# Two-stream modulations as products on TensorE in a bank of their own, loads two steps ahead, five banks in the long feed forwards, Toeplitz products interleaved

## The chip, the cores and the metric

The kernel runs on one core of one Trainium2 chip. The metric is the device time of one execution in microseconds (us); less is better.

## The reference

Four layers (pool, attention, state space, gated MLP), each followed by a convolutional feed forward. Each of the layers takes six modulation vectors out of one matrix product with the conditioning vector, and in the first two layers the latent stream of 256 positions and the context stream of 256 positions both run through everything; in the last two only the latent stream does.

```python
sh1, sc1, gt1, sh2, sc2, gt2 = ada_modulations(c, ada_w[layer], ada_b[layer])      # silu(c) @ w + b, split in 6
csh1, csc1, cgt1, csh2, csc2, cgt2 = ada_modulations(c_ctx, ada_w[layer], ada_b[layer])
...
x_lat = post_norm_residual(x_lat, y_lat, gt1, ln1_g[layer], ln1_b[layer])
f_lat = conv_ffn(modulate(x_lat, sh2, sc2), ffn_w_up[layer], ffn_conv_w[layer], ffn_conv_b[layer], ffn_w_down[layer])
...
def conv_ffn(h, w_up, conv_w, conv_b, w_down):
    a = h @ w_up                                   # [n, 1024] @ [1024, 5632]
    a = conv_b + ap[:, 0:n] * conv_w[0] + ...      # three taps along the positions
    val, gate = a[..., :FFN_HIDDEN], a[..., FFN_HIDDEN:]
    return (val * jax.nn.silu(gate)) @ w_down      # [n, 2816] @ [2816, 1024]
```

`ada_w` is 4 x 1024 x 6144 and all of it has to be read. The state-space layer (64 groups of 16 channels, 64 complex states, both directions) is computed by the kernel as long convolutions in blocks. Their kernels are made beforehand from the layer's parameters; one part of that, for each of 8 blocks of channels and each half of 4 groups, is a set of small products, the Toeplitz products.

## The kernel before

**Matrix products.** Each float32 product is done as three reduced products of a high and a low part (`mm3`, lines 223 to 225; `hH`, `hL` are the parts of the activations, `wH`, `wL` those of the weights). A weight block of 128x1024 is loaded into `raw`, ScalarE writes `wH` (line 164), VectorE or GpSimd the difference `wL` (line 165).

**The feed forward** (`ffn`) goes over 11 pairs of 128 hidden channels, in three parts. For each pair, 4 accumulators of one bank each (`ps`; value half `vi` 0 and gate half `vi` 1, each of two channel tiles) take 96 ordinary products of 512 columns. Behind them stand the convolution (ScalarE's Identity on line 1794, VectorE's lines 1795 and 1797, all from the bank into `cv`), Silu, the product of the halves on GpSimd (line 1801) and the split into `gH`, `gL`. After each part come the down products, whose results VectorE adds through `tmp` (lines 406 and 407). The banks of PSUM are shared out by `banks(n)`: 6 for `ps`, two (`bg`) for background work. Each of the two stages for layers 0 and 1 has 66 weight blocks; after each block's load stands a `hook`.

**Background work.** At each hook, `bg` takes steps of two lists, by a rate. The first list are modulation tasks (l, m) (`ada_task`): one step loads 128 rows of one of the six blocks of `ada_w` (`araw`, 512 KB). Task (0,5) multiplies them on TensorE (`products`, line 310: four column groups of 32, 256 columns each, which the trace counts as 8 records). Tasks of layers 1 to 3 instead sum on VectorE, with the conditioning value as scalar (line 323 for the first step, line 325 for the others, once for each stream, into `adaS`), and products with a vector of ones close the sum. Tasks (1,0) to (1,4) fall into the first feed forward, (1,5) and (2,0) to (2,4) into the second. The second list prepares the state-space layer (`ssm_tasks`): GpSimd makes complex products `ef` and `efp` (lines 1160 to 1167), from which `toeplitz` makes one call of products for each of 8 blocks and 2 halves.

**Order.** The program's order of writing is not the order on the engines: a scheduler with a cost model of its own lists the instructions of each engine, and each engine then works its list in order. Waits for data and for free buffers come on top.

In the middle of the first pair of a long feed forward, `turn_second` transposes the second stream (`turn`), with banks from the same six.

Of the kernel before, what the change touches and what calls it, by code (L numbers as in the profile page):

```python
# [65 lines left out]
class Trunk:  # L66
    def __init__(self, ctx, tc, I, out, out_ctx=None, layers=(0, 1, 2, 3)):
# [3 lines left out]
        self.pp, self.bgp, self.held, self.ada, self.begun = [], None, [], {}, set()  # L71
# [35 lines left out]
    def banks(self, n, bg=2):  # L107


        self.flush()  # L110
        for pool in reversed(self.held):
            pool.release()
        self.held, self.pp, self.bgp, self.psn = [], [], None, 0
        self.more_banks(0, bg)
        self.more_banks(n)

# [8 lines left out]
    def flush(self):  # L125

        if self.bg_ada and self.bg_ada[0][0] in self.begun and not self.alone(*self.bg_ada[0][0]):
            self.need(self.bg_ada[0][0])
# [164 lines left out]


# [3 lines left out]
    def ada_task(self, l, m, place=None, scale=None, vec=None, bank=None, apart=False):  # L298
# [6 lines left out]
        bank = bank or (lambda: self.ps(True))  # L305
        vec = not l == 0 if vec is None else vec
        ps = None
        def products(lhs, rhs, start, stop):
            for q in range(4):
                nc.tensor.matmul(ps[32 * q:32 * q + 32, 0:256], lhsT=lhs, rhs=rhs[:, q * 256:(q + 1) * 256], start=start, stop=stop)  # L310
        two = vec and not self.alone(l, m)
        acc = [self.t(self.sm, [128, D], F32, "adaS", 2) for r in range(1 + two)] if vec else None
        for k in range(KT):
            raw = place(128)
            self.last_load = nc.sync.dma_start(raw, I["ada_w"][l, k * 128:(k + 1) * 128, m * D:(m + 1) * D])
            if acc is None:
                ps = ps or bank()
                products(self.cond[:, k, :], raw, k == 0, k == KT - 1 and not gate)
            else:
                with self.tc.issue_after(self.last_hT.ins):  # L320
                    for r, a in enumerate(acc):
                        if k == 0:
                            nc.vector.tensor_scalar(a, raw, self.cond[:, k, r:r + 1], None, op0=ALU.mult)
                        else:
                            nc.vector.scalar_tensor_tensor(a, raw, self.cond[:, k, r:r + 1], a, op0=ALU.mult, op1=ALU.add)  # L325
            if k < KT - 1:
                yield
# [200 lines left out]
    def turn(self, r):  # L528

        pss = []  # L530
        for kk in range(4):
            if kk == 2 and r:

                self.psn -= 2
# [794 lines left out]
    def ssm_pre(self, k, pp, eng, behind):  # L1329
# [33 lines left out]
        def toeplitz(hb, f):  # L1363
            nc.sync.dma_start(self.fD[k, :, hb], f.rearrange("p r n -> p (r n)"))
            pk = [self.ps(True), self.ps(True)]
            for q in range(4):
                g = 4 * hb + q
                rows = slice(32 * q, 32 * q + 32)
                lhs = lambda i, hp: pr[hp, self.XB + i * 128 + g * 16:self.XB + i * 128 + g * 16 + 32]
                for i in range(2):  # L1370
                    mm(pk[0][rows, 0:112], lhsT=lhs(i, slice(64, 128)), rhs=f[64:128, i, q * 128 + 16:q * 128 + 128], start=i == 0, stop=i == 1)
                for i in range(2):
                    mm(pk[1][rows, 128:240], lhsT=lhs(i, slice(0, 64)), rhs=f[0:64, i, q * 128:q * 128 + 112], start=i == 0, stop=i == 1)
                for i in range(2):
                    mm(pk[1][rows, 112:128], lhsT=lhs(i, slice(0, 128)), rhs=cs[:, i, g], start=i == 0, stop=False)
# [377 lines left out]
    def ffn(self, l, last):  # L1753
# [8 lines left out]
        with tc.tile_pool(name=f"ffn{l}", bufs=2) as fp:  # L1762
            for part, pairs in enumerate(parts):
                gs = []
                for p in pairs:
# [3 lines left out]
                    pss = [[self.ps() for j in range(2)] for vi in range(2)]  # L1769
                    ws = {}  # L1770

                    for r, vi in ((0, 0), (0, 1), (1, 1), (1, 0))[:2 * S] if p == 0 else ((None, 0), (None, 1)):
# [12 lines left out]
                    cw = cw or self.conv(l)  # L1785
                    for j in range(2):
                        hid = 2 * p + j
                        cv = []
                        for vi in range(2):
                            ps = pss[vi][j]  # L1790
                            h = hid + vi * NHT
                            c = self.t(fp, [128, S, 256], F32, f"cv{vi}", 2)
                            p3 = ps[:, :T].rearrange("p (s n) -> p s n", s=S)
                            nc.scalar.activation(c, p3, AF.Identity, scale=cw[:, 1, h:h + 1], bias=cw[:, 3, h:h + 1])  # L1794
                            nc.vector.scalar_tensor_tensor(c[:, :, 1:], p3[:, :, :255], cw[:, 0, h:h + 1], c[:, :, 1:],  # L1795
                                                           op0=ALU.mult, op1=ALU.add)
                            nc.vector.scalar_tensor_tensor(c[:, :, :255], p3[:, :, 1:], cw[:, 2, h:h + 1], c[:, :, :255],  # L1797
                                                           op0=ALU.mult, op1=ALU.add)
                            cv.append(c)
                        nc.scalar.activation(cv[1], cv[1], AF.Silu)  # L1800
                        nc.gpsimd.tensor_tensor(cv[0], cv[0], cv[1], op=ALU.mult)  # L1801
                        gH = self.t(fp, [128, T], F32R, "gH", 8)
                        gL = self.t(fp, [128, T], F32R, "gL", 8)
                        c0 = cv[0].rearrange("p s n -> p (s n)")
# [103 lines left out]
    def run(self):  # L1908
# [10 lines left out]
        for l in ls:  # L1919
# [3 lines left out]
            if l < 2 and todo:  # L1923
                self.rate, self.until = ((0.85, 0.85)[l], 2.0), (l + 1, 4)
# [5 lines left out]
            if l == 2 and 3 in ls:  # L1930
                self.gmlp_open()
            self.ffn(l, l == ls[-1])
# [33 lines left out]
```

## Time and profile before

| | |
|---|---|
| Median of three runs | 1969.92 us (1967.69 to 1974.09) |
| The profiled execution's own time | 1976.77 us |
| Its span in the trace | 1975.0 us |
| TensorE (PE) busy | 1796.1 us, 91% of the span |
| VectorE (DVE) busy | 1489.5 us, 75% |
| GpSimd (POOL) busy | 1131.2 us, 57% |
| ScalarE (ACT) busy | 780.9 us, 40% |
| Mean granted clock of TensorE | 0.953 |

The shares are means over stages that differ. The first feed forward runs from about 80 to 545 us, the second from about 760 to 1215 us. In the rows, PE is TensorE's matmuls and PEld its weight loads, L310 is line 310 of the kernel, and `a<-b,c` says which tile is written from which.

### The profile page before, as it was taken

The numbers are of one execution on the slowest core, as the hardware profiler recorded it, in microseconds if no ns is written. First come the engines' busy times: TensorE is split into PE (matmuls) and PEld (weight loads), VectorE is DVE, ScalarE is ACT, GpSimd is POOL, SyncE is SP. The second block draws the span as 40 slices with busy tenths as digits, with TensorE's granted clock in tenths as the row PEclk, the third lists the DMA queues.
The fourth block names the chain that finished last, engine by engine and source line by source line (L and its number), as shares of the span: only waits on it lengthen the run. The fifth ranks groups of instructions, "written<-read, shape, count | busy, mean of one in ns | idle before, by whom it ended". The sixth has DMA issues, their size and how long they took to land.

```text
span 1975.0 us, 31117 instructions
## 1 busy us (share of the span) xinstructions
PE 1796.1 (91%) x11804; PEld 1496.4 (76%) x11804; DVE 1489.5 (75%) x1981; ACT 780.9 (40%) x1288; POOL 1131.2 (57%) x1040
## 2 busy tenths in 40 slices
PE   6899999898999998988999998679898988979997
PEld 4787787676788877766877677448897968979997
DVE  4676997895777767978866546987889798778666
ACT  3252243124346643332432232234544544436553
POOL 1477218999763326852168996756654554236543
PEclk9899999998999999999999999888999999989999
DMA  9465665654321122546655647775878856447652
GB/s 354 165 195 185 204 213 166 202 177 136 106 90 32 44 88 55 202 125 208 223 195 202 208 138 232 209 220 181 277 259 270 279 198 210 156 144 268 212 183 86
DMA packets 241784, 360.25 MB, mean 182 GB/s; under 512 B 43353, under 2 KB 164825, under 8 KB 241634
## 3 DMA queue, kind: packets, MB, share of 16 engines
q1 hardware_dynamic: 241634, 358.26, 56.0%
q8 instruction: 93, 1.52, 0.3%
q14 instruction: 57, 0.47, 0.1%
HBM read 330.92 MB, written 27.29 MB: 181 GB/s over the span
## 4 chain that ended last, share of the span: by engine, by line
PE 27%; POOL 13%; DVE 9%; DMA 6%; issue 3%; ACT 1%; SPq 0%; POOLq 0%; DVEq 0%; ACTq 0%
PE ps L225 8%; PE ps L223 8%; PE ps L224 8%; DMA araw<-in_ada_w_dram 2%; DVE wL L165 2%; DVE adaS L325 1%; DMA raw<-in_ffn_w_up_dram 1%; POOL cv L1801 1%; POOL ef L1165 1%; POOL efp L1166 1%; POOL ef L1160 1%; POOL ef L1162 1%; POOL efp L1161 1%; POOL ef L1167 1%; POOL wL L165 1%
## 5 line engine op out<-in xcount | busy, mean ns | idle before, releaser
L223 PE MATMUL ps<-hH,wH 128*128 128x256 f32 (+1 forms) x1568 | 525.4, 337 | 26.2 <-DVE cv L1797 9.6
L225 PE MATMUL ps<-hH,wL 128*128 128x256 f32 (+1 forms) x1568 | 520.4, 333 | 7.4 <-DVE wL L165 7.4
L224 PE MATMUL ps<-hL,wH 128*128 128x256 f32 (+1 forms) x1568 | 522.0, 333 | 0.8 <-DVE hL L512 0.7
L164 ACT ACTIVATE wH<-raw 128x1024 fp32r<-128x1024 f32 x341 | 358.0, 1056 | 400.5 <-PE ps L225 190.9
L165 DVE TENSOR_TENSOR wL<-raw,wH 128x1024 fp32r<-128x1024 f32 x292 | 424.8, 1461 | 114.0 <-ACT wH L164 104.1
L223 PEld LDWEIGHTS ps<-hH,wH 128*128 128x128 f32 x1568 | 305.2, 195 | 59.3 <-issue 12.6
L225 PEld LDWEIGHTS ps<-hH,wL 128*128 128x128 f32 x1568 | 304.8, 195 | 35.6 <-DVE wL L165 8.6
L224 PEld LDWEIGHTS ps<-hL,wH 128*128 128x128 f32 x1568 | 305.9, 195 | 26.5 <-POOL xa L617 0.9
L325 DVE SCALAR_TENSOR_TENSOR adaS<-araw,cond,adaS 128x1024 f32<-128x1024 f32 x182 | 282.8, 1572 | 42.4 <-DMA araw<-in_ada_w_dram 42.0
L1801 POOL TENSOR_TENSOR cv<-cv,cv 128x512 f32<-128x512 f32 (+1 forms) x88 | 119.2, 1360 | 224.8 <-ACT cv L1800 218.1
L224 PE MATMUL ps<-wL,gH 128*128 128x512 f32 (+1 forms) x552 | 216.4, 393 | 11.9 <-DVE wL L165 11.9
L223 PE MATMUL ps<-wH,gH 128*128 128x512 f32 (+1 forms) x552 | 216.6, 395 | 5.9 <-DVE tmp L406 5.5
L225 PE MATMUL ps<-wH,gL 128*128 128x512 f32 (+1 forms) x552 | 211.8, 391 | 4.4 <-DVE gL L1806 3.8
L165 POOL TENSOR_TENSOR wL<-raw,wH 128x1024 fp32r<-128x1024 f32 x49 | 125.1, 2555 | 115.1 <-ACT wH L164 97.4
L1794 ACT ACTIVATE cv<-ps,cw 128x512 f32<-128x512 f32 (+1 forms) x176 | 115.3, 665 | 139.8 <-PE ps L225 104.7
L1795 DVE SCALAR_TENSOR_TENSOR cv<-ps,cw,cv 128x510 f32<-128x510 f32 (+1 forms) x176 | 106.0, 608 | 62.3 <-ACT cv L1794 59.6
L224 PEld LDWEIGHTS ps<-wL,gH 128*128 128x128 f32 x552 | 105.6, 191 | 36.2 <-DVE wL L165 14.7
L223 PEld LDWEIGHTS ps<-wH,gH 128*128 128x128 f32 x552 | 105.5, 191 | 32.2 <-DVE tmp L406 6.0
L225 PEld LDWEIGHTS ps<-wH,gL 128*128 128x128 f32 x552 | 105.2, 191 | 28.7 <-DVE gL L1806 4.9
L524 POOL TENSOR_SCALAR rs<-mv 128x1 f32<-128x1 f32 x26 | 8.2, 314 | 176.1 <-DVE mv L522 175.8
L1797 DVE SCALAR_TENSOR_TENSOR cv<-ps,cw,cv 128x510 f32<-128x510 f32 (+1 forms) x176 | 105.9, 611 | 3.0
L1805 ACT ACTIVATE gH<-cv 128x512 fp32r<-128x512 f32 (+1 forms) x88 | 45.8, 522 | 131.7 <-POOL cv L1801 131.7
(414 smaller groups left out, 3471.7 us busy)
## 6 DMA issues: line engine op xcount, KB each, us to landing
araw<-in_ada_w_dram SPq DMA_DIRECT2D x184, 512.0 KB
raw<-in_ffn_w_up_dram SPq DMA_DIRECT2D x176, 512.0 KB
raw<-in_ffn_w_down_dram SPq DMA_DIRECT2D x88, 512.0 KB
raw<-in_gmlp_w_in_dram SPq DMA_DIRECT2D x32, 512.0 KB
fD<-ef SPq DMA_DIRECT2D x16, 512.0 KB
eD<-eo SPq DMA_DIRECT2D x16, 512.0 KB
raw<-in_gmlp_w_out_dram SPq DMA_DIRECT2D x16, 512.0 KB
raw<-in_attn_w_qkv_dram SPq DMA_DIRECT2D x12, 512.0 KB
```

Source lines behind the costliest of these rows:

```text
L164: self.nc.scalar.activation(h, x, AF.Copy)
L165: (eng or self.nc.vector).tensor_tensor(l, x, h.bitcast(F32), op=ALU.subtract)
L223: mm(ps, lhsT=w[0], rhs=x[0], start=first, stop=False)
L224: mm(ps, lhsT=w[0], rhs=x[1], start=False, stop=False)
L225: mm(ps, lhsT=w[1], rhs=x[0], start=False, stop=last)
L325: nc.vector.scalar_tensor_tensor(a, raw, self.cond[:, k, r:r + 1], a, op0=ALU.mult, op1=ALU.add)
L1160: eng.tensor_tensor(out[0], a[0], b[0], op=ALU.mult)
L1794: nc.scalar.activation(c, p3, AF.Identity, scale=cw[:, 1, h:h + 1], bias=cw[:, 3, h:h + 1])
L1795: nc.vector.scalar_tensor_tensor(c[:, :, 1:], p3[:, :, :255], cw[:, 0, h:h + 1], c[:, :, 1:], op0=ALU.mult, op1=ALU.add)
L1797: nc.vector.scalar_tensor_tensor(c[:, :, :255], p3[:, :, 1:], cw[:, 2, h:h + 1], c[:, :, :255], op0=ALU.mult, op1=ALU.add)
L1801: nc.gpsimd.tensor_tensor(cv[0], cv[0], cv[1], op=ALU.mult)
L1805: nc.scalar.activation(gH, c0, AF.Copy)
```

## The change

- `array(l, m)` names the tasks that are multiplied on TensorE: now those of layers 0 and 1 and (2,0) to (2,4). For these `lag` is 2 outside the pool layer: step k loads rows k and multiplies rows k - 2, so a task takes ten steps. The rate of steps a hook goes from 0.85 to 1.05.
- The feed forwards of layers 0 and 1 have 5 banks for `ps` (`ffn_banks`) and one for the modulations.
- `convolve(vi)` is written right behind the products of each half, and the banks of the second half are claimed when its products begin. `turn_second` there has four banks of its own choosing.
- `toeplitz` puts the two row halves and the four column groups in alternation instead of one column group after the other; the sums for each element are the same.

```diff
+    def ffn_banks(self):
+
+        self.banks(5)
+        self.adab_pool = self.tc.alloc_tile_pool(name=self.uid("adap"), bufs=1, space=PSUM)
+        self.held.append(self.adab_pool)
...
+    def array(self, l, m):
+
+        return l < 2 or l == 2 and m < 5
...
-        vec = not l == 0 if vec is None else vec
+        vec = not self.array(l, m) if vec is None else vec
+        lag = 0 if vec or l == 0 and m < 5 else 2
...
-        for k in range(KT):
-            raw = place(128)
-            self.last_load = nc.sync.dma_start(raw, I["ada_w"][l, k * 128:(k + 1) * 128, m * D:(m + 1) * D])
+        for k in range(KT + lag):
+            if k < KT:
+                raws.append(place(128))
+                self.last_load = nc.sync.dma_start(raws[k], I["ada_w"][l, k * 128:(k + 1) * 128, m * D:(m + 1) * D])
             if acc is None:
                 ps = ps or bank()
-                products(self.cond[:, k, :], raw, k == 0, k == KT - 1 and not gate)
+                if k >= lag:
+                    products(self.cond[:, k - lag, :], raws[k - lag], k == lag, k == KT + lag - 1 and not gate)
...
-            for q in range(4):
-                g = 4 * hb + q
...
+            for i in range(2):
+                for g, q, rows in gq:
+                    mm(pk[0][rows, 0:112], lhsT=lhs(i, g, slice(64, 128)), rhs=f[64:128, i, q * 128 + 16:q * 128 + 128], start=i == 0, stop=i == 1)
+                    mm(pk[1][rows, 128:240], lhsT=lhs(i, g, slice(0, 64)), rhs=f[0:64, i, q * 128:q * 128 + 112], start=i == 0, stop=i == 1)
+            for i in range(2):
+                for g, q, rows in gq:
+                    mm(pk[1][rows, 112:128], lhsT=lhs(i, g, slice(0, 128)), rhs=cs[:, i, g], start=i == 0, stop=False)
+            for g, q, rows in gq:
...
-                    pss = [[self.ps() for j in range(2)] for vi in range(2)]
+                    pss, ws, cv = [None, None], {}, {}
+                    def convolve(vi):
...
+                        pss[vi] = pss[vi] or [self.ps() for j in range(2)]
-                        if (r, vi) == (0, 1):
+                        if (r, vi) == (0, 1) and self.second:
+                            free = iter([self.ps(), self.t(self.adab_pool, [128, 512], F32, "ada")] + [self.ps(True) for _ in range(2)])
+                            self.turn_bank = lambda: next(free)
                             self.turn_second()
+                            self.turn_bank = None
...
+                        cw = cw or self.conv(l)
+                        if vi not in [v for _, v in steps[si + 1:]]:
+                            convolve(vi)
...
-                self.rate, self.until = ((0.85, 0.85)[l], 2.0), (l + 1, 4)
+                self.rate, self.until = (1.05, 2.0), (l + 1, 4)
...
+            if l < 2:
+                self.ffn_banks()
```

The new lines shift those behind them: 223 to 225 become 229 to 231, 310 becomes 321, 164 becomes 170, and the lines of `ffn` and `toeplitz` move likewise.

TensorE's list in the first feed forward, where the down products of its first part begin. Before, the up products of one pair are followed by down products (`ps_1753`) with nothing between:

```order
L224 MATMUL ps_1511<-hL_106,wH_1643 128x512
L225 MATMUL ps_1511<-hH_105,wL_1644 128x512
L223 MATMUL ps_1753<-wH_1737,gH_1088 128x512
L224 MATMUL ps_1753<-wL_1738,gH_1088 128x512
L225 MATMUL ps_1753<-wH_1737,gL_1089 128x512
L223 MATMUL ps_1753<-wH_1737,gH_1102 128x512
```

In the changed kernel a step of task (1,0) stands between them (`ada_1648` is its accumulator), and the next one 18 products later:

```order
L230 MATMUL ps_1623<-hL_106,wH_1683 128x512
L231 MATMUL ps_1623<-hH_105,wL_1684 128x512
L321 MATMUL ada_1648<-araw_1646,cond_94 32x256 x4
L229 MATMUL ps_1765<-wH_1747,gH_1107 128x512
L230 MATMUL ps_1765<-wL_1748,gH_1107 128x512
```

Such a step now stands after most blocks of 24 ordinary products of both feed forwards.

TensorE's list at one Toeplitz call in the first feed forward (`bg_3318` and `bg_3319` are the call's two banks, `prm` the parameters). Before, each column group's products of 64 rows are followed by its small ones:

```order
L1371 MATMUL bg_3318<-ef_3184,prm_3178 32x112 x2
L1373 MATMUL bg_3319<-ef_3184,prm_3178 32x112 x2
L1375 MATMUL bg_3319<-prm_3178 32x16 x2
L1377 MATMUL bg_3319<-dg_3180,ident_81 16x16
L1371 MATMUL bg_3318<-ef_3184,prm_3178 32x112 x2
```

In the changed kernel all products of 64 rows come first, in alternation between the banks, and the small ones of the four groups stand together at the end (the last four of sixteen products of 64 rows are shown):

```order
L1386 MATMUL bg_3348<-ef_3208,prm_3202 32x112
L1387 MATMUL bg_3349<-ef_3208,prm_3202 32x112
L1386 MATMUL bg_3348<-ef_3208,prm_3202 32x112
L1387 MATMUL bg_3349<-ef_3208,prm_3202 32x112
L1390 MATMUL bg_3349<-prm_3202 32x16 x8
L1393 MATMUL bg_3349<-dg_3204,ident_81 16x16 x4
L230 MATMUL ps_3386<-wL_3334,gH_2347 128x512
```

ScalarE's list at the start of the second feed forward. Before, the two activations that read `th` (the sine for the state-space layer's parameters) stand ahead of the ones that empty the first pair's banks into `cv`:

```order
L164 ACTIVATE wH_7647<-raw_7645 128x1024
L1228 ACT_TABLE_LOAD
L1228 ACTIVATE un_1349_7859<-th_7812 128x32
L1229 ACTIVATE kk_7852<-th_7812 128x32
L1794 ACTIVATE cv_1294_7585<-ps_7327,cw_7080 128x512
L164 ACTIVATE wH_7679<-raw_7677 128x1024
L1794 ACTIVATE cv_1298_7599<-ps_7328,cw_7080 128x512
```

In the changed kernel the first pair's banks come first:

```order
L170 ACTIVATE wH_7700<-raw_7698 128x1024
L1792 ACTIVATE cv_1289_7588<-ps_7430,cw_7122 128x512
L170 ACTIVATE wH_7742<-raw_7740 128x1024
L1792 ACTIVATE cv_1290_7592<-ps_7431,cw_7122 128x512
L1822 ACT_TABLE_LOAD
L1822 ACTIVATE cv_1289_7588<-cv_1289_7588 128x512
L1792 ACTIVATE cv_1291_7644<-ps_7380,cw_7122 128x512
L1792 ACTIVATE cv_1292_7648<-ps_7381,cw_7122 128x512
```

There the two that read `th` (lines 1243 and 1244 now) follow twenty rows later, behind the activations of two further halves.

## Rows read from the trace of the kernel before

**Rows 1.** The page: busy time of TensorE and TensorE's weight loads, all engines.

```profile
PE 1796.1 (91%) x11804; PEld 1496.4 (76%) x11804; DVE 1489.5 (75%) x1981; ACT 780.9 (40%) x1288; POOL 1131.2 (57%) x1040
```

**Rows 2.** Windows by stage, both feed forwards: us, busy us by engine, clock, DMA.

```profile
100.00:545.00 445.00, 419.17 (x2295) 327.54 (x2296) 351.95 (x387) 149.68 (x214) 311.08 (x299) 0.97 0.56 176
...
760.00:1215.00 455.00, 417.51 (x2259) 331.86 (x2258) 326.66 (x369) 142.63 (x206) 294.87 (x286) 0.96 0.56 180
```

**Rows 3.** TensorE's waits, 100 to 545 us: total, times, longest.

```profile
PE bg L1371 <- POOL ef L1167: 8.8, 4, 5.9
PE ps L223 <- DVE tmp L406: 5.5, 1, 5.5
PE ps L224 <- DVE wL L165: 4.4, 3, 1.9
```

**Rows 4.** TensorE's waits, 760 to 1215 us.

```profile
PE ps L223 <- DVE cv L1797: 9.0, 1, 9.0
PE bg L1371 <- POOL ef L1167: 7.9, 4, 2.6
PE ps L224 <- DVE wL L165: 7.5, 3, 3.7
PE bg L1371 <- POOL ef L1162: 4.7, 3, 2.2
PE ps L225 <- DVE wL L165: 2.9, 2, 2.5
```

**Rows 5.** Windows: ten low-clock stretches of both feed forwards, the first and the sum.

```profile
366.60:373.40 6.80, 5.56 (x16) 3.28 (x18) 6.80 (x7) 0.00 (x0) 6.57 (x5) 0.50 0.61 178
...
sum 61.20, PE 50.89 PEld 37.59 DVE 45.43 ACT 12.53 POOL 46.87; mean PE 5.09 PEld 3.76 DVE 4.54 ACT 1.25 POOL 4.69
```

**Rows 6.** Windows: a stretch in which GpSimd makes ef.

```profile
300.00:500.00 200.00, 180.08 (x1094) 137.86 (x1093) 154.47 (x127) 59.98 (x91) 189.17 (x121) 0.95 0.52 168
```

**Rows 7.** Timeline of TensorE around one modulation step: start, duration, what.

```profile
143.49 0.39 PE L224 MATMUL ps<-hL,wH 128*128 128x512 f32 x1
143.72 0.39 PE L225 MATMUL ps<-hH,wL 128*128 128x512 f32 x1
144.03 0.64 PE L310 MATMUL bg<-araw,cond 128*32 128x256 f32 x8
144.60 0.50 PE L223 MATMUL ps<-hH,wH 128*128 128x512 f32 x1
```

**Rows 8.** Timeline of TensorE: products that close a sum made on VectorE.

```profile
270.43 1.07 PE L310 MATMUL bg<-adaS,ones 128*32 128x256 f32 x16
271.43 0.50 PE L223 MATMUL ps<-hH,wH 128*128 128x512 f32 x1
```

**Rows 9.** The page's groups: VectorE's modulation operation.

```profile
L325 DVE SCALAR_TENSOR_TENSOR adaS<-araw,cond,adaS 128x1024 f32<-128x1024 f32 x182 | 282.8, 1572 | 42.4 <-DMA araw<-in_ada_w_dram 42.0
```

**Rows 10.** Timeline of GpSimd: one operation, twice.

```profile
330.35 1.06 POOL L1160 TENSOR_TENSOR ef<-prm 128x512 f32<-128x512 f32 x1
...
338.16 2.05 POOL L1166 TENSOR_TENSOR efp<-prm 128x512 f32<-128x512 f32 x1
```

**Rows 11.** Timeline of ScalarE at the start of the second feed forward.

```profile
787.68 0.23 ACT L1228 ACTIVATE un<-th 128x32 f32<-128x32 f32 x1 [7.87 <-DVE th L1226]
...
787.93 0.76 ACT L1794 ACTIVATE cv<-ps,cw 128x512 f32<-128x512 f32 x1
```

**Rows 12.** Timeline of TensorE: one Toeplitz call, its first round, its end.

```profile
501.92 0.40 PE L225 MATMUL ps<-wH,gL 128*128 128x512 f32 x1
502.25 0.28 PE L1371 MATMUL bg<-ef,prm 64*32 64x112 f32 x1
...
502.76 0.30 PE L1375 MATMUL bg<-prm 128*32 128x16 f32 x4
...
503.04 0.28 PE L1371 MATMUL bg<-ef,prm 64*32 64x112 f32 x1
...
505.41 0.50 PE L223 MATMUL ps<-wH,gH 128*128 128x512 f32 x1
```

More of the change, by code (lines that the diff above doesn't have):

```diff
@@ L70, in __init__ @@
         self.n = 0
-        self.pp, self.bgp, self.held, self.ada, self.begun = [], None, [], {}, set()
+        self.pp, self.bgp, self.adab_pool, self.held, self.ada, self.begun = [], None, None, [], {}, set()
         self.bg_ada, self.bg_pre = [], []
@@ L112, in banks @@
             pool.release()
-        self.held, self.pp, self.bgp, self.psn = [], [], None, 0
+        self.held, self.pp, self.bgp, self.adab_pool, self.psn = [], [], None, None, 0
         self.more_banks(0, bg)
         self.more_banks(n)
+    def ffn_banks(self):
+        self.banks(5)
+        self.adab_pool = self.tc.alloc_tile_pool(name=self.uid("adap"), bufs=1, space=PSUM)
+        self.held.append(self.adab_pool)
     def more_banks(self, n, bg=0):
@@ L125, in flush @@
     def flush(self):
-        if self.bg_ada and self.bg_ada[0][0] in self.begun and not self.alone(*self.bg_ada[0][0]):
+        if self.bg_ada and self.bg_ada[0][0] in self.begun and self.array(*self.bg_ada[0][0]):
             self.need(self.bg_ada[0][0])
@@ L304, in ada_task @@
         place = place or (lambda rows: self.t(self.wp, [rows, D], F32, "araw", 3))
-        bank = bank or (lambda: self.ps(True))
-        vec = not l == 0 if vec is None else vec
+        bank = bank or (lambda: self.t(self.adab_pool, [128, 512], F32, "ada") if self.adab_pool else self.ps(True))
+        vec = not self.array(l, m) if vec is None else vec
         ps = None
+        lag = 0 if vec or l == 0 and m < 5 else 2
         def products(lhs, rhs, start, stop):
@@ L322, in ada_task @@
                         if k == 0:
[L323 removed]
+                            nc.vector.tensor_scalar(a, raws[k], self.cond[:, k, r:r + 1], None, op0=ALU.mult)
                         else:
[L325 to L326 removed]
+                            nc.vector.scalar_tensor_tensor(a, raws[k], self.cond[:, k, r:r + 1], a, op0=ALU.mult, op1=ALU.add)
+            if k < KT + lag - 1:
                 yield
@@ L531, in turn @@
         for kk in range(4):
-            if kk == 2 and r:
+            if kk == 2 and r and not self.turn_bank:
                 self.psn -= 2
@@ L1365, in toeplitz @@
             pk = [self.ps(True), self.ps(True)]
-            for q in range(4):
-                g = 4 * hb + q
[L1368 to L1375, printed above, removed]
+            gq = [(4 * hb + q, q, slice(32 * q, 32 * q + 32)) for q in range(4)]
+            lhs = lambda i, g, hp: pr[hp, self.XB + i * 128 + g * 16:self.XB + i * 128 + g * 16 + 32]
+            for i in range(2):
[6 more added lines that the diff above has]
+            for g, q, rows in gq:
                 gc = slice(16 * g, 16 * g + 16)
@@ L1784, in ffn @@
                                              self.hT(4 * kk + k, cs), kk == 0 and k == 0, kk == 1 and k == 3)
-                    cw = cw or self.conv(l)
+                        cw = cw or self.conv(l)
+                        if vi not in [v for _, v in steps[si + 1:]]:
+                            convolve(vi)
                     for j in range(2):
[L1787 to L1801, printed above, removed]
+                        c0 = cv[0, j].rearrange("p s n -> p (s n)")
+                        nc.scalar.activation(cv[1, j], cv[1, j], AF.Silu)
+                        nc.gpsimd.tensor_tensor(cv[0, j], cv[0, j], cv[1, j], op=ALU.mult)
                         gH = self.t(fp, [128, T], F32R, "gH", 8)
                         gL = self.t(fp, [128, T], F32R, "gL", 8)
-                        c0 = cv[0].rearrange("p s n -> p (s n)")
                         nc.scalar.activation(gH, c0, AF.Copy)
```

14 lines of the change are left out of this document (12 added, 2 removed).

## The prediction

> **What bounds the kernel now.** I read the page first: TensorE is busy 91% of the span [rows 1], so the kernel is as long as TensorE's list of products plus whatever interrupts it. The change touches the feed forwards of layers 0 and 1, so the next view was the span by stage. Those two stages take 445 and 455 us; in each TensorE is busy some 418 us and VectorE 352 and 327, GpSimd 311 and 295 [rows 2]. The reader is to see two things: TensorE has only 26 and 37 us without work there, and VectorE and GpSimd are loaded enough to be late now and then.
>
> Then the waits of TensorE in both stages. In the first they are few and long: 8.8 us for GpSimd's `ef`, one of 5.5 us for a bank that `tmp` still reads, 4.4 us for `wL` [rows 3]. In the second, one of 9.0 us for a bank held by `cv`, 10.4 us in two rows for `wL`, 12.6 us for `ef` [rows 4]. A wait costs more than itself: ten stretches of the two stages, 61.2 us together, ran at a granted clock of 0.50, the lower of its two levels (the first, from 366.6 us, begins at the end of the wait for `tmp`). TensorE was busy for 50.9 us of them [rows 5], and at the full clock that work takes half as long, so they cost at most 25.4 us.
>
> Last, where `ef` is made: between 300 and 500 us GpSimd is busy 189 of 200 us [rows 6]. There GpSimd is the engine nearest its limit, not TensorE (180). This is the main doubt below.
>
> **Modulations to TensorE.** Eleven tasks, (1,0) to (1,5) and (2,0) to (2,4), change from a sum on VectorE to products: 8 steps each, 88 steps of four products (eight records). One such step stands in the trace, since (0,5) does it already. The product before it starts at 143.72, the next one behind it at 144.60, where ordinary products follow each other every 0.23 us [rows 7]: 0.88 - 0.23 = 0.65 us a step, and 88 x 0.65 = +57.2 us. What goes from TensorE are the closing products on the sums: 1.00 us from the first record to the next ordinary product [rows 8], against 144.60 - 144.03 = 0.57 in a step, so 0.65 + 0.43 = 1.08 us for each of the eight two-stream tasks; for the three of one stream I take a step's 0.65. That is 8.6 + 2.0 = 10.6 us less. **Sum: +46.6 us on TensorE.** Nothing hides it, except where TensorE waits anyway.
>
> VectorE loses 16 operations for each of the eight tasks and 8 for each of the three, 152 in all, at 1572 ns [rows 9]: 239 us, 120 to 130 of them in each of the two stages. By itself that is worth nothing; it pays through waits, and through GpSimd: its 128x512 operation takes 1.06 us at 330.35 and 2.05 us at 338.16 [rows 10]. What doubles it is not in these rows; that it is VectorE's work beside it is my reading.
>
> *Waits on VectorE.* `tmp` 5.5 and `wL` 4.4, 7.5 and 2.9 are late because VectorE is behind [rows 3, 4]. The 9.0 us for `cv` have another cause: ScalarE stood 7.87 us on `th`, the sine of the state-space parameters [rows 11], with the activations that empty the banks queued behind it. The order of the changed kernel puts that sine behind the next pairs' activations, so this wait goes for its place, not its load. I take `tmp` and `cv` whole (14.5) and two thirds of the three `wL` (9.9, since a third of VectorE's load goes and only these are marginal): **-24.4 us**; bounds -12 (`cv`'s and 3 more) and -29.3 (all five).
>
> *Waits on GpSimd.* 8.8 + 7.9 + 4.7 = 21.4 us for `ef` [rows 3, 4]. With a third of VectorE's work gone, operations nearer to 1.06 than to 2.05 us become more frequent, but TensorE also asks sooner. Half: **-10.7 us**; bounds 0 and -21.4.
>
> *Clock.* 35.1 of the 50.7 us of listed waits go by the above, so up to 0.69 of 25.4 us; some of the low stretches hold no large wait, so I take **-15 us**, bounds -3 and -25.
>
> **Loads two steps ahead.** A step's product runs when its rows were issued two steps earlier. The price is ten steps a task instead of eight; the rate goes from 0.85 to 1.05 a hook, 60 steps in a feed forward's 66 hooks, so tasks still end in their stage. No further load is issued. I put it at nothing: what hides a load is two steps, some 11 us of products. If that cover failed, each late row would stop TensorE itself, where before it only stopped VectorE.
>
> **Toeplitz products.** Sixteen calls of 56 records. In one call, the last ordinary product starts at 501.92 and the next at 505.41 [rows 12]: 3.49 - 0.23 = 3.26 us. It is four equal rounds of 0.79 us, one for each column group, and a round is 0.51 us for the 64-row products (502.25 to 502.76) and 0.28 us for six small ones (502.76 to 503.04). Interleaved, all four groups are in flight at once. That groups overlap is seen in [rows 7]: eight records of 256 columns, four groups, take the 0.57 us of two passes. So I expect 0.33 to start, 0.65 for the thirty-two 64-row records, 0.65 for the twenty-four small ones, less 0.23: 1.4 us. **Saved: 1.9 us a call, -30.5 us.** Bounds: if the small ones stay one behind another, 24 x 0.28/6 = 1.1 us, the call takes 1.8 us and the saving is 23 us; if they overlap as fully as the large, 0.3 us, it is 35.
>
> The Trainium skill (TensorEngine Tiling (Array Packing), Instruction Overhead) says that every matmul costs about 60 cycles however few its columns, and that no tiling factor should be taken from a dimension that is already small; that speaks against gaining anything on the 16-column products. An estimate by it (25 ns for each of 56 records at 2.4 GHz, one behind another) gives a call of 1.5 us, a saving of some 28 us and a sum 2 us longer than mine. In [rows 12] records of the two row halves start 0.01 us apart, so the trace does not bear out that every record occupies the whole engine that long.
>
> **Banks and convolution.** Five banks in place of six, an accumulator bank for the modulations, and the convolution of each half of a pair behind that half's products. The next pair's first half takes the spare bank and one whose convolution began half a pair (some 11 us) earlier; emptying a bank starts with an activation of 0.76 us [rows 11]. It should be covered. The transposes of the second stream now stand together at the start of a feed forward. I allow **+4 us** for such waits; bounds 0 and the third rival's 33.
>
> **Sum.** 46.6 - 30.5 - 24.4 - 10.7 - 15 + 4 = -30.0 us. The profiled execution took 1976.8 us (span 1975.0), the median of three runs is 1969.9, so the execution that I read is 7 us long; I apply the difference to the median: **1940 us.** A measurement of this kernel can tell about 0.3%, 6 us, from no change.
>
> **Rivals.** *Everything goes.* All bounds at their best: 46.6 - 35 - 29.3 - 21.4 - 25 = -64, 1906 us. For it: VectorE would be far from its limit. Against it: GpSimd's list of operations is not shorter. I give 1906 to 1930 a chance of 0.17.
>
> *GpSimd bounds the stretch of [rows 6] and its like in the second feed forward.* Then what TensorE saves on Toeplitz products it waits for `ef` again; the modulation steps in these stretches (some 40 of 88, by their share of the stages) are hidden too. Left: 48 x 0.65 - 10.6 = 20.6, less 24.4, less 8 of the clock, plus 4: -8 us, 1962 us. For it: 189 of 200 us. Against it: those are operations stretched by VectorE. Chance 0.16, for 1955 to 1970.
>
> *Slower: banks run short.* With one spare bank, each of the 22 pairs makes TensorE wait until two activations of 0.76 us are through: 22 x 1.5 = 33 us, and the clock's 15 us are not given back, since short waits come more often. -30 + 33 - 4 + 15 = +14, 1984 us. It decides from about 1.4 us a pair. Against it: the 11 us of cover. Chance 0.13.
>
> **How the numbers follow.** The forecast, 1930 to 1955, has 0.52; 0.02 are left for a change of order that I have not seen. Below 1964 lie the forecast, the first rival and half of the second: 0.77. Within 6 us of 1970: the rest of the second and a little of the third, 0.10. Slower 0.13. The range leaves out the best part of the first rival and the third: 1914 to 1970; the forecast's own is 1930 to 1955.
>
> **What would show it.** VectorE some 120 us less busy in each of the two stages, TensorE's modulation products at 0.6 to 0.7 us a step; a Toeplitz call between ordinary products of 1.3 to 1.8 us instead of 3.5; no wait for `cv` at the second feed forward's start and none for `tmp`; waits for `ef` about halved, GpSimd's operations shorter; fewer half-clock stretches. I am wrong if the waits for `ef` grow by what the Toeplitz calls lose, if TensorE waits for `araw` or for `cv` pair after pair, or if a step costs over 0.9 us.

## The result, and the profile after

The changed kernel takes 1937.06 us (median of 4 runs, 1934.53 to 1942.82) against 1970.58 us before (4 runs). The ratio is 0.983, with a 95% interval of 0.9813 to 0.9848: 33.5 us less, where 1940 us (1914 to 1970) was forecast. The two profiled executions took 1976.8 and 1936.8 us, 40 us apart, since that of before was a long one; readings of the traces below add up to the 40.

The page after, span and busy times by engine:

```profile
span 1935.0 us, 32041 instructions
...
PE 1785.0 (92%) x12356; PEld 1459.8 (75%) x12356; DVE 1285.8 (66%) x1829; ACT 782.2 (40%) x1289; POOL 1071.9 (55%) x1040
```

TensorE has hardly less to do in all, VectorE 204 us less. By stage, with windows whose ends lie as far from each feed forward's last down product as those of [rows 2] (columns as there):

```profile
100.00:533.50 433.50, 419.38 (x2561) 316.68 (x2560) 242.89 (x308) 150.78 (x214) 279.66 (x304) 0.99 0.58 180
748.50:1176.40 427.90, 416.83 (x2577) 316.08 (x2576) 232.39 (x296) 143.56 (x207) 266.81 (x286) 0.99 0.61 188
```

The first stage is 11.5 us shorter, the second 27.1: together 38.6 of the 40. TensorE is without work for 14 and 11 us of them, where it was 26 and 37. VectorE is 109 and 94 us less busy, and GpSimd 31 and 28, although GpSimd has 1040 operations in the whole kernel before and after.

TensorE's waits in the two windows (total, times, longest), to be put beside [rows 3, 4]; the first stage:

```profile
PE bg L1386 <- POOL ef L1177: 5.1, 1, 5.1
PE bg L1405 <- POOL ef L1182: 3.1, 2, 2.3
PE ps L229 <- DVE cv L1795: 2.6, 1, 2.6
PE bg L1386 <- POOL ef L1182: 2.2, 3, 1.1
```

The second:

```profile
PE bg L1386 <- POOL ef L1177: 5.0, 2, 4.7
PE ps L229 <- DVE cv L1795: 2.5, 1, 2.5
PE bg L1386 <- POOL ef L1182: 2.2, 3, 1.1
PE bg L1405 <- POOL ef L1182: 0.8, 1, 0.8
```

No row for `tmp` or `wL` is left, and the 9.0 us for `cv` at the second feed forward's start are gone. A new short wait for `cv`, 2.6 and 2.5 us, stands once in each, at the first down product (194.4 and 853.3 us), which needs a bank that is still being read into `cv`. The waits for `ef` are what remains: 18.4 us, and they were 24.3 (21.4 in [rows 3, 4], and 2.9 in smaller rows of the same views).

One Toeplitz call, its first products, its small ones and the next ordinary product (beside [rows 12]):

```profile
480.35 0.39 PE L231 MATMUL ps<-hH,wL 128*128 128x512 f32 x1
480.67 0.28 PE L1386 MATMUL bg<-ef,prm 64*32 64x112 f32 x1
480.68 0.28 PE L1387 MATMUL bg<-ef,prm 64*32 64x112 f32 x1
...
481.21 0.32 PE L1390 MATMUL bg<-prm 128*32 128x16 f32 x16
481.36 0.22 PE L1393 MATMUL bg<-dg,ident 128*16 128x16 f32 x8
481.51 0.50 PE L229 MATMUL ps<-hH,wH 128*128 128x512 f32 x1
```

And one modulation step (beside [rows 7]):

```profile
146.65 0.39 PE L231 MATMUL ps<-hH,wL 128*128 128x512 f32 x1
146.97 0.64 PE L321 MATMUL ada<-araw,cond 128*32 128x256 f32 x8
147.54 0.50 PE L229 MATMUL ps<-hH,wH 128*128 128x512 f32 x1
```

The call went from 3.26 us net to 1.16 - 0.23 = 0.93, the step costs 0.89 - 0.23 = 0.66. These are the prices where nothing interrupts: eight of the sixteen calls take 1.15 to 1.16 us, the others are split by an ordinary product or hold a wait.

Half-clock stretches of both stages, four now (beside [rows 5]):

```profile
376.50:383.30 6.80, 5.01 (x63) 3.26 (x64) 0.00 (x0) 0.54 (x2) 6.31 (x6) 0.50 0.43 128
...
sum 20.40, PE 16.78 PEld 11.79 DVE 6.67 ACT 5.10 POOL 17.09; mean PE 4.19 PEld 2.95 DVE 1.67 ACT 1.28 POOL 4.27
```

20.4 us in place of 61.2, of which TensorE is busy for 16.8. Each of the four stands at the end of one of the four longest waits above: 2.6 and 2.5 us for `cv`, 5.1 and 4.7 us for `ef`.

### The profile page after: what moved, and what is told of

Its sections match the earlier page's. It is cut to its first block, busy times and chain, and to the rows that moved or that the text cites. A ratio compares the mean times of both kernels' runs of the same rounds, so it can differ in the third digit from the quotient of the medians.

```text
span 1935.0 us, 32041 instructions
## 1 busy us (share of the span) xinstructions
PE 1785.0 (92%) x12356; PEld 1459.8 (75%) x12356; DVE 1285.8 (66%) x1829; ACT 782.2 (40%) x1289; POOL 1071.9 (55%) x1040
## 4 chain that ended last, share of the span: by engine, by line
PE 53%; POOL 17%; DVE 13%; DMA 6%; issue 5%; ACT 3%; SPq 0%; POOLq 0%; DVEq 0%; ACTq 0%
PE ps L229 14%; PE ps L230 13%; PE ps L231 13%; DVE wL L171 3%; POOL cv L1823 2%; PE ada L321 2%; DVE adaS L340 2%; DMA araw<-in_ada_w_dram 1%; POOL xa L633 1%; PE sc L990 1%; PE ps L938 1%; POOL ef L1177 1%; PE pv L1045 1%; DMA prm<-prmD 1%; POOL ef L1180 1%
## 5 line engine op out<-in xcount | busy, mean ns | idle before, releaser
L171 DVE TENSOR_TENSOR wL<-raw,wH 128x1024 fp32r<-128x1024 f32 x292 | 430.1, 1477 | 252.0 <-ACT wH L170 235.4
L229 PE MATMUL ps<-hH,wH 128*128 128x256 f32 (+1 forms) x1568 | 523.1, 335 | 16.8 <-DVE gvec L245 6.6
L230 PE MATMUL ps<-hL,wH 128*128 128x256 f32 (+1 forms) x1568 | 516.4, 330 | 1.7 <-DVE hL L527 1.1
L229 PEld LDWEIGHTS ps<-hH,wH 128*128 128x128 f32 x1568 | 300.7, 192 | 61.4 <-issue 12.2
L231 PEld LDWEIGHTS ps<-hH,wL 128*128 128x128 f32 x1568 | 300.9, 192 | 31.9 <-DVE wL L171 5.0
L230 PEld LDWEIGHTS ps<-hL,wH 128*128 128x128 f32 x1568 | 301.8, 192 | 26.1 <-POOL xa L632 1.3
L1823 POOL TENSOR_TENSOR cv<-cv,cv 128x512 f32<-128x512 f32 (+1 forms) x88 | 111.7, 1275 | 221.2 <-ACT cv L1822 220.9
L1015 POOL TENSOR_SCALAR araw<-araw,den 128x512 f32<-128x512 f32 (+1 forms) x64 | 40.9, 654 | 86.0 <-ACT gate L1032 21.8
```

Of the source, the lines that this page charges most:

```text
L171: (eng or self.nc.vector).tensor_tensor(l, x, h.bitcast(F32), op=ALU.subtract)
L229: mm(ps, lhsT=w[0], rhs=x[0], start=first, stop=False)
L230: mm(ps, lhsT=w[0], rhs=x[1], start=False, stop=False)
L231: mm(ps, lhsT=w[1], rhs=x[0], start=False, stop=last)
L1015: nc.gpsimd.tensor_scalar(pt[:, e, i], pt[:, e, i], den[:, e, i:i + 1], 1.0, op0=ALU.mult, op1=ALU.mult)
L1823: nc.gpsimd.tensor_tensor(cv[0, j], cv[0, j], cv[1, j], op=ALU.mult)
```

## The experiments

Each was timed beside the kernel before on the same chip; a ratio is to that kernel, with its 95% interval.

**e1, the Toeplitz products alone.** The kernel before with the new `toeplitz`:

```diff
-            for q in range(4):
-                g = 4 * hb + q
...
+            for i in range(2):
+                for g, q, rows in gq:
...
```

Expected: 

> The kernel before with the interleaved Toeplitz products and nothing else. Theory A (TensorE's list is the bound, and what a call loses the span loses): a call costs 0.93 us instead of 3.26 beside ordinary products, 16 calls, 37 us less, so 1933 us against 1970, between 1930 and 1942. Theory B (GpSimd bounds the stretches with the Toeplitz calls): TensorE waits for ef by what the calls lose, the waits for ef grow from 24 us to over 45, and the time is 1960 to 1970.

Measured: 1960.38 us, ratio 0.9942 (0.9927 to 0.9957). TensorE's waits between 84 and 545 us:

```profile
PE bg L1371 <- POOL ef L1167: 12.7, 5, 5.2
...
PE bg L1390 <- POOL ef L1167: 2.3, 1, 2.3
PE bg L1371 <- POOL ef L1162: 1.8, 2, 0.9
...
PE bg L1390 <- POOL ef L1162: 1.3, 1, 1.3
```

and between 740 and 1215 us:

```profile
PE bg L1371 <- POOL ef L1167: 14.3, 5, 5.4
...
PE bg L1390 <- POOL ef L1167: 6.2, 3, 3.0
...
PE bg L1371 <- POOL ef L1162: 2.2, 2, 1.6
```

TensorE's list is 37 us shorter, and the kernel 11 us. Waits for `ef` grew from 24.3 to 40.8 us in these rows: theory B, by the time and by the kind of wait; the 45 us that it asked for were not reached.

**e2, all but the Toeplitz products.** The changed kernel with the old `toeplitz` (the diff of e1, reversed).

Expected: 

> The changed kernel with the Toeplitz products in the old order, one column group after the other. Theory A: 37 us more than the changed kernel's 1937, so 1974 us (1968 to 1980), which says that the rest of the change is worth about nothing. Theory B: GpSimd hides the slower calls, 1940 to 1950, and the rest of the change is what pays.

Measured: 1955.03 us, ratio 0.9914 (0.9891 to 0.9938). Neither number: by the ratios the rest of the change is worth 17 us by itself, and the new products another 17 with it. The waits for `ef` are nearly gone here; in both feed forwards together:

```profile
PE bg L1386 <- POOL ef L1182: 3.7, 3, 1.7
...
PE bg L1386 <- POOL ef L1177: 0.7, 2, 0.5
```

So VectorE's relief, together with the steps on TensorE, took the waits for `ef` from 24.3 us to 4.4, and the faster calls put 14 back. Alone the two halves give 11 and 17 us, together 33.5; by the intervals (some 3 us each way for the first, 5 for the second) that is not clearly more than their sum.

**e3, all but the modulations on TensorE.** The rule by which `flush` ends a task is that of before, too (not shown).

```diff
     def array(self, l, m):
-        return l < 2 or l == 2 and m < 5
+        return l == 0
...
-                self.rate, self.until = (1.05, 2.0), (l + 1, 4)
+                self.rate, self.until = (0.85, 2.0), (l + 1, 4)
```

Expected: 

> The changed kernel, but the eleven tasks stay sums on VectorE at the old rate of 0.85 (five banks, the early convolution and the interleaved Toeplitz products stay). Theory A (by the sum of the prediction, 46.6 us of products against 50 us of waits and of half clock): about 1940 us, 1932 to 1948. Theory B (the waits were a matter of order and banks, not of VectorE's load): 46 us less than the changed kernel, 1890 to 1905. Theory C (VectorE's load makes more waits the faster TensorE gets): 1950 to 1965.

Measured: 1979.53 us (1970.25 to 1982.09), ratio 1.0024 (1.0007 to 1.004): no faster than the kernel before, and beyond all three theories; with everything else in place, the modulations on TensorE are worth some 40 us. In the profiled executions, 45 us apart, e3 is 15 us later at the end of the first feed forward, 30 at that of the second, and the last 15 are lost behind it, where the two kernels run the same code. The waits for `ef` in the two feed forwards are 37.0 us, twice those of the changed kernel. The largest single wait stands in the second:

```profile
PE ps L229 <- ACT wH L170: 17.7, 2, 17.4
PE bg L1386 <- POOL ef L1182: 12.4, 6, 3.7
PE bg L1405 <- POOL ef L1182: 4.8, 3, 2.0
```

ScalarE's timeline at that place:

```profile
889.37 0.63 ACT L1826 ACTIVATE gH<-cv 128x512 fp32r<-128x512 f32 x1 [18.22 <-POOL cv L1823]
889.90 0.61 ACT L1822 ACTIVATE cv<-cv 128x512 f32<-128x512 f32 x1
893.29 0.63 ACT L1826 ACTIVATE gH<-cv 128x512 fp32r<-128x512 f32 x1 [2.78 <-POOL cv L1823]
893.83 2.94 ACT L170 ACTIVATE wH<-raw 128x1024 fp32r<-128x1024 f32 x3
```

The activation that makes `wH` stands in ScalarE's list behind one that waits 18.2 us for GpSimd's `cv`, which has the state-space parameters ahead of it. That wait comes from the order of the lists.

**e10, which part of e3 costs.** The kernel before with the new `toeplitz` and the early `convolve`, six banks:

```diff
+                        if vi not in [v for _, v in steps[si + 1:]]:
+                            convolve(vi)
```

Expected: 

> The kernel before with the interleaved Toeplitz products and the early convolution, six banks, sums on VectorE. It stands between the kernel with new Toeplitz products alone (1960 us) and the one with five banks as well (1979.5 us). Theory A (it is the five banks that cost 19 us while VectorE is loaded): 1957 to 1964. Theory B (it is the early convolution's place in the lists): 1974 to 1982.

Measured: 1962.07 us, ratio 0.9951 (0.9934 to 0.9968), no different from e1: theory A by the time. So what e3 loses comes with the five banks and the modulations' own; no run tells whether by a lack of banks or by the order that the scheduler made of it. The wait above does not settle it: of the two profiled executions, 26 us apart, both take 668 us from the end of the first feed forward to that of the second, with that wait and without. e3 is 11 us longer in the first feed forward and 15 behind the second. In the first, TensorE is idle as long in both (38 and 37 us) but slower in e3, at a mean granted clock of 0.94 against 0.97.

**e4, the old convolution in the changed kernel.**

```diff
-                        if vi not in [v for _, v in steps[si + 1:]]:
-                            convolve(vi)
...
+                    pss = [[self.ps() for j in range(2)] for vi in range(2)]
```

Expected: 

> The changed kernel with all four banks of a pair claimed at once and the convolution of both halves behind the pair, as before; five banks, modulations on TensorE and interleaved Toeplitz products stay. Theory A (a bank is free in time either way, since a half pair of products covers it): 1934 to 1942 us. Theory B (with five banks the late convolution makes each of the 22 pairs wait about 1.5 us): 1960 to 1975, with waits of TensorE for cv or for the activation at each pair.

Measured: 1935.8 us, ratio 0.9813 (0.9796 to 0.983): no difference from the changed kernel. Theory A.

**e5, VectorE's relief by itself.**

```diff
-                        else:
+                        elif not (l < 2 or l == 2 and m < 5):
                             nc.vector.scalar_tensor_tensor(a, raw, self.cond[:, k, r:r + 1], a, op0=ALU.mult, op1=ALU.add)
```

Expected: 

> The kernel before, without VectorE's accumulating operations of the eleven tasks (seven of eight steps of their sums are left out, so the modulations are incomplete; loads, the first step and the closing products stay). TensorE's list is that of before, VectorE has some 210 us less. It measures what VectorE's relief is worth by itself. Theory A: modulations on TensorE without new Toeplitz products gained 16 us and cost 46.6 us of products, so relief is worth 63 us: 1908 us (1900 to 1918). Theory B: the waits come from order and banks, which this kernel does not change: 1940 us or more.

Measured: 1908.04 us, ratio 0.9671 (0.9652 to 0.969): 64 us, as theory A had it. The first feed forward in it:

```profile
84.00:531.00 447.00, 437.33 (x2545) 352.31 (x2545) 270.62 (x356) 163.21 (x238) 301.90 (x316) 1.00 0.56 181
```

The granted clock is 1.00 there. Up to the end of the second feed forward, TensorE, with the same list, is without work for 45 us less than in the kernel before and busy for 27 us less, nearly all of it half clock given back. The longest of its waits for `ef` in the first feed forward is

```profile
PE bg L1371 <- POOL ef L1162: 3.1, 1, 3.1
```

and all of them are 6.6 us in both stages. In the second, the wait for `cv` behind the sine has stayed

```profile
PE ps L223 <- DVE cv L1797: 8.8, 1, 8.8
```

so VectorE's load was not its cause. How GpSimd's operation on `ef` changes when only VectorE's sums go, between 84 and 531 us, is seen in this group of the kernel before

```profile
L1162 POOL TENSOR_TENSOR ef<-ef,efp 128x512 f32<-128x512 f32 x20 | 35.2, 1759 | 0.7
```

and in the same of e5

```profile
L1162 POOL TENSOR_TENSOR ef<-ef,efp 128x512 f32<-128x512 f32 x20 | 31.3, 1565 | 0.7
```

and of the changed kernel:

```profile
L1177 POOL TENSOR_TENSOR ef<-ef,efp 128x512 f32<-128x512 f32 x20 | 31.2, 1562 | 0.8
```

1759 ns, then 1565 and 1562: the same operation, 20 times in the stage. It is one of six such groups. All six took 190.1 us in the first feed forward before, 164.1 in e5 and 163.7 in the changed kernel; in the second 171.2, 163.5 and 164.0, where this one group did not become shorter (1412, 1527 and 1539 ns). So VectorE's sums cost GpSimd's `ef` operations 26 us in the first feed forward and 7 to 8 in the second.

**e6, the products' price by itself.**

```diff
-                    products(self.cond[:, k - lag, :], raws[k - lag], k == lag, k == KT + lag - 1 and not gate)
+                    if lag == 0 or l == 0 or k == lag:
+                        products(...)
```

Expected: 

> The changed kernel with one of eight product steps in each of the eleven tasks (77 of 88 steps left out, so the modulations are incomplete; all loads stay). It measures the price of the products. Theory A: every step costs its 0.66 us on the path that sets the end: 77 x 0.66 = 51 us less than 1937, 1886 us (1880 to 1893). Theory B: in the stretches where GpSimd is nearest its limit the steps are hidden, some 40 of 88: 1905 to 1915, and the waits for ef grow by 20 us or more.

Measured: 1901.15 us, ratio 0.9631 (0.9613 to 0.965): 36 us less than the changed kernel by the medians, 39 by the ratios, between the theories. Its waits for `ef` in the first feed forward:

```profile
PE bg L1387 <- POOL ef L1183: 5.3, 2, 3.5
PE bg L1406 <- POOL ef L1183: 3.9, 4, 1.4
PE bg L1387 <- POOL ef L1178: 3.6, 2, 2.8
```

12.8 us against 10.4 (in the second 10.9 against 8.0), and its clock in both stages (the third column from the end):

```profile
84.00:531.00 447.00, 424.98 (x2491) 343.00 (x2492) 267.08 (x347) 163.08 (x238) 300.86 (x315) 0.97 0.56 181
740.00:1180.00 440.00, 410.41 (x2535) 329.17 (x2537) 263.83 (x346) 151.45 (x228) 304.83 (x324) 0.96 0.64 206
```

0.97 and 0.96 where the changed kernel has 0.98 and 0.99 in the same windows: 12 to 15 of the 51 us are taken back, by waits and the lower clock. Theory B's 20 us more of waits for `ef` did not come; they grew by 5.

e6 beside e5 shows the worth of the faster Toeplitz calls once more: neither has VectorE's accumulating operations nor, but for 11 steps, the products in their place (e6 has the five banks and the early convolution, too). TensorE's list is some 40 us shorter in e6 (37 by the calls, 11 by the closing products, less 7 for the 11 steps), and e6 is 8 us faster by the ratios. The first feed forward ends no sooner (510.3 and 508.1 us); its waits for `ef` are 12.8 us in place of 4.5, its clock 0.97 in place of 1.00 in the window 84 to 531.

**e7, two steps' products at once** (one step less a task, rate 0.95):

```diff
-                if k >= lag:
-                    products(self.cond[:, k - lag, :], raws[k - lag], ...)
+                if two_k and k and k % 2 == 0:
+                    for kk in (k - 2, k - 1):
+                        products(self.cond[:, kk, :], raws[kk], kk == 0, kk == KT - 1 and not gate)
```

Expected: 

> The changed kernel with the products of two steps together at every second load (nine steps a task, rate 0.95). Two steps together cost 1.32 - 0.23 = 1.09 us against 2 x 0.66: 44 x 0.23 = 10 us less than 1937. Theory A (all of it on the path): 1927 us, 1923 to 1932. Theory B (GpSimd or the loads take it back): 1933 to 1942.

Measured: 1942.8 us (1935.24 to 1943.01), ratio 0.9831 (0.9808 to 0.9853), no gain. In the profiled execution, the longest of five, the second feed forward ended 8.6 us earlier than the changed kernel's; up to the end of the third 7.5 were lost again, and behind it another 7. The third has waits for `cv`:

```profile
PE ps L229 <- DVE cv L1798: 8.0, 4, 5.7
```

which are 1.2 us in the changed kernel. But TensorE's idle time there is nearly the same in all (9.2 us in the changed kernel, 10.9 in e7); what grew is its busy time, 172.8 to 179.1, at a lower clock. The changed kernel's third feed forward, and that of e7:

```profile
1362.00:1544.00 182.00, 172.83 (x1205) 155.73 (x1205) 159.02 (x185) 94.10 (x145) 98.36 (x62) 0.99 0.79 269
```

```profile
1352.00:1542.00 190.00, 179.08 (x1220) 161.40 (x1221) 158.30 (x183) 94.07 (x145) 100.97 (x61) 0.96 0.77 260
```

Nothing of the edit runs there; the lists are in another order.

**e9, no lag.**

```diff
-        lag = 0 if vec or l == 0 and m < 5 else 2
+        lag = 0
...
-                self.rate, self.until = (1.05, 2.0), (l + 1, 4)
+                self.rate, self.until = (0.85, 2.0), (l + 1, 4)
```

Expected: 

> The changed kernel with each product in the step of its own load (no lag, eight steps a task, rate 0.85). Theory A (the lag hides the load, and without it TensorE's list, worked in order, stops for araw): waits for araw of 10 us or more in the two feed forwards, 1945 to 1960 us. Theory B (the scheduler places the product late enough by itself): 1933 to 1941 us.

Measured: 1944.3 us, ratio 0.9869 (0.9848 to 0.989); the interval touches that of the changed kernel. In both long feed forwards TensorE has no wait for `araw`, with the lag or without, and they end within 2 us of the changed kernel's. The difference in the profiled executions lies in the third, again (6 us up to its end), and behind it (4 us). The third has little more idle time (10.0 us) and a lower clock than the changed kernel's:

```profile
1365.00:1552.00 187.00, 177.03 (x1204) 161.04 (x1203) 156.31 (x181) 92.80 (x143) 95.32 (x59) 0.96 0.76 256
```

Theory A is refuted as to its cause; B's range is missed by 3 us.

**e11 and e8, a third of the `ef` work on VectorE,** once in the kernel before and once in the changed one:

```diff
-        eng.tensor_tensor(out[0], out[0], t, op=ALU.subtract)
+        (last or eng).tensor_tensor(out[0], out[0], t, op=ALU.subtract)
...
-        eng.tensor_tensor(out[1], out[1], t, op=ALU.add)
+        (last or eng).tensor_tensor(out[1], out[1], t, op=ALU.add)
...
-            yield from self.cmul_steps(out, a, b, [128, *dims], eng, tag="efp", bufs=1, pool=pp)
+            yield from self.cmul_steps(out, a, b, [128, *dims], eng, tag="efp", bufs=1, pool=pp, last=nc.vector)
```

Expected of the kernel before: 

> The kernel before with the last operation of each part of the ef products on VectorE, so GpSimd has a third less of ef work and VectorE some 80 operations more. Theory A (in the kernel before it is GpSimd's lateness that costs most): 1945 to 1960 us. Theory B (it is VectorE's own lateness): waits for wL, tmp and cv grow, 1972 to 1990 us.

Measured: 1959.82 us, ratio 0.9944 (0.9925 to 0.9963). Its waits in the second feed forward:

```profile
PE ps L223 <- DVE cv L1797: 8.6, 1, 8.6
PE ps L224 <- DVE wL L165: 8.1, 3, 3.1
...
PE ps L225 <- DVE wL L165: 3.3, 2, 2.5
PE bg L1371 <- DVE ef L1167: 2.2, 1, 2.2
```

The waits for `ef` are almost gone (4.1 us in both stages, where they were 24.3). Those for `wL` doubled in the first feed forward, 4.4 to 8.8 us, and did not change in the second (11.4 against 11.2 in the same window). Both theories hold a part, and GpSimd's lateness weighs more: 11 us less, although VectorE has more to do.

Expected of the changed kernel: 

> The changed kernel, with the last operation of each part of the ef products (a third of GpSimd's ef work) on VectorE. Theory A (GpSimd's load is what the remaining 18 us of waits for ef come from, and VectorE has room now): the waits fall below 6 us, 1922 to 1930 us. Theory B (the two engines lengthen each other whichever of them runs an operation, or the hand-over between them costs as much): 1934 to 1945.

Measured: **1923.65 us** (1922.1 to 1925.14), ratio 0.9749 (0.973 to 0.9767): better than both kernels. In both feed forwards one short wait for `ef` is left:

```profile
PE ps L229 <- DVE cv L1795: 2.7, 1, 2.7
...
PE bg L1386 <- DVE ef L1182: 0.6, 1, 0.6
```

## Why the prediction was right

The sum held, and each term went the way that was forecast. Several sizes were off, and that their errors nearly cancel is luck.

- **Modulations to TensorE, +46.6 us.** 88 steps of 0.66 us, less the closing products: 47.5 us of TensorE's list. What they cost the end is less: by e6, 36 to 39 us for the 77 steps that were left out, 0.5 a step. That is the part of the second rival that was true.
  VectorE is 204 us less busy; the 152 operations at their mean were 239. That reading was too high: 19 of the 152 are first steps of a sum, which took 1058 ns and not 1572, and the records that went are 222 us in sum. The rest is the way of counting: VectorE's records overlap (1601 us of records in 1489 us of busy time before), and busy time counts an overlap once. By stage it is 109 and 94 us where 120 to 130 was forecast.
- **Waits on VectorE, -24.4 us: mis-sized.** All five waits, 29.3 us, went, the bound and not the estimate. The sine's part went for its place in the list, as said: in e5, without VectorE's sums, the 8.8 us for `cv` are still there. It is not the early convolution that moved it, for e10 has the wait (8.6 us) and e4 has not.
- **Toeplitz products, -30.5 us: mis-sized.** The call costs 0.93 us where 1.4 was forecast, so TensorE's list lost 16 x 2.33 = 37 us, beyond the bound of 35. The sixteen pairs of 64 rows take 0.54 us (480.67 to 481.21) where I had 0.65, and the 24 small ones 0.30 us where I had 0.65: 12.5 ns each. The Trainium skill's overhead for a matmul (TensorEngine Tiling (Array Packing), Instruction Overhead), which I had estimated as 25 ns for each record, one behind another, gives 0.6 us for the 24; the trace shows half of that, so in four column groups they are not one behind another.
- **Waits on GpSimd, -10.7 us: mis-sized the other way.** 24.3 us became 18.4, so -5.9. By e5 the relief alone takes 18 us of them, by e2 it takes 20 together with the steps on TensorE, and the faster calls put 14 back, since they ask for `ef` sooner. The two errors nearly cancel: -41.2 forecast for both, -43 measured.
- **Clock, -15 us.** At half clock TensorE was busy for 16.8 us in place of 50.9, so the loss went from 25.4 to 8.4 us: -17.
- **Loads two steps ahead, nothing; banks and convolution, +4 us.** e9 shows no wait for `araw` either way, e4 no difference by the convolution. The +4 is the new wait for `cv` at the first down product, 5.1 us in both stages; two of the four half-clock stretches stand at it. That five banks cost no more is read from the changed kernel's trace; no run has that kernel with six, and with VectorE's sums, e3 and e10 are some 15 us apart.

47.5 - 29.3 - 37 - 5.9 - 17 + 5.1 = -37 of the 38.6 us by which the two stages shrank. That it comes so close is in part luck as well: by the windows, TensorE's idle time fell by 38 us, where the waits above make 30, and its busy time by less than 1, where the list and the clock make 6.5.

Of the rivals, *everything goes* and *slower* did not come; *GpSimd bounds* holds for either half of the change alone. That is the main finding: the relief is worth 64 us by itself (e5), where my three terms for it gave 50; the products on TensorE take 36 to 47 of it back; and the Toeplitz calls' 37 us reach the end only in part: 11 us (3 each way) in the kernel before, 17 (6 each way) in the changed one, and some 8 us for a list that is 40 us shorter in e6 beside e5. What is missing went into waits for `ef` and the half clock behind them. GpSimd is nearer to keeping up because its operations become shorter when VectorE runs fewer. This is measured: in e5 nothing else was changed, and the time from the start of an `ef` operation to that of the next one right behind it is 1548 ns in the mean over both stages before, 1393 in e5 and 1389 in the changed kernel. From 84 us to the end of the first feed forward GpSimd's idle time did not fall (137 us before, 138 in e5), so it is not that GpSimd waited less. In the second feed forward these operations are only 7 to 8 us shorter while the waits for `ef` fell by 12; that part is not explained in full. That the two engines hinder each other at the memory's ports, as the Trainium skill has it (SBUF — State Buffer, SBUF: two separate sides), agrees with the shorter operations; no run here isolates the port.

What stays open: why the stretch from the end of the second feed forward to that of the third, whose code is not touched in e7 and e9, is 6 to 8 us longer there. Its lists are in another order than the changed kernel's, and in e4 and e8, where the order is nearly the changed kernel's, it takes the same time within 1 us. The time is lost at the half clock and not in longer waits. But the changed kernel's own executions lie 8 us apart (1934.53 to 1942.82), and one execution of each kernel was traced, so that the order is the cause is likely and not shown.

## What to carry to other kernels

Work that is taken from an engine that is not the bound can pay more than the price of doing it on the one that is (here 64 us against 36 to 47): count the waits that it causes, the half clock behind them, and the time it adds to its neighbour's operations. A gain in products that wait for another engine's results is worth only what that engine can follow; look at its busy share in that stretch first, and relieve it in the same change (e8 took another 13 to 16 us that way). A difference of some 8 us can lie in a stage that no edit touched, by the order of the lists or the granted clock; find the stage in the trace before a cause is named.

## What the runs showed of the hardware

In one Toeplitz call, thirty-two records of 64 rows, in two row halves and four column groups, and 24 small ones in the four groups take 0.84 us together in alternation, where one group after the other took 3.16; the 24 small ones start 12.5 ns apart on average, where six of one group took 0.28 us, 47 ns each. GpSimd's six kinds of `ef` operations (128x512) took 190 us in the first feed forward beside VectorE's sums and 164 without them; in the second it was 171 and 164.
